# Preparing the first projection of a three-mixer block: modulation rows on the tensor engine, one rms pass, the low halves on VectorE

## The chip, the cores and the metric

The kernel runs on one core of one Trainium2 chip. The metric is the device time of one execution in microseconds; lower is better. Of three runs of the kernel before the median is 1512.63 us.

## The reference, cut to what matters

A block with attention is followed by two mixers (a gated convolution and an mLSTM). The change touches only the front end of the first block, where `x` is 512 x 1024 and `w_in` has 1024 rows:

```python
mod = c @ w_ada + b_ada                      # c: 1 x 1024, w_ada: 1024 x 3072
shift, scale, gate = split(mod, 3)
h = rms_norm(x, g_pre) * (1 + scale) + shift # per channel; rms per token
proj = h @ w_in
```

All is float32. A large product is made from three products of rounded halves: high x high, high x low, low x high. Every operand of such a product therefore has to be split into a high half (rounded by ScalarE) and a low half (value minus high half).

## The kernel before

`x` is held transposed: eight tiles of 128 channels by 512 tokens (`x1[:, k]`). For every tile `k` the kernel needs two columns of 128 numbers, `Gc[:, k]` = (1 + scale) * g_pre and `Sc[:, k]` = shift, and the inverse rms of each token, spread over all partitions (`rbc`, 128 x 512). From them comes the normalised tile `h`, split into `hh[:, k]` and `hl[:, k]` (in the trace `uh` and `ul`, whose memory they share).

*The modulation.* `ada_load(k)` fetches a 1 MB tile of `w_ada` (eight blocks of 128 x 256: 128 columns of scale beside 128 of shift) into one of three buffers `ada`. `ada_mac(k)` multiplies block `q` with the per-partition scalar `c` and adds up on VectorE: two TENSOR_SCALAR, six SCALAR_TENSOR_TENSOR and one TENSOR_TENSOR, all 128 x 256, into tiles `mac`. `modmm(k, m)` adds over partitions with two small matmuls against a column of ones, and two VectorE instructions make `Gc` and `Sc`.

*The rms.* `x` arrives in two halves of 256 tokens, four pieces each. For each half ScalarE squares eight tiles, VectorE adds them, `stat_cols` sums over partitions with matmuls, takes the root (ScalarE) and the reciprocal (VectorE), and `cols_bc` spreads the result by diagonal matrices and matmuls into `rbc`. Tiles 0 and 1 of `x` are multiplied by `rbc` on VectorE, tiles 2 to 7 on GpSimd.

*The tile.* `mkh(k)` runs ScalarE twice over the scaled tile (once rounding into `hh`, once exact into `t`), and VectorE subtracts to `hl`.

*The weights.* `Weights` streams units of the weights (here 128 x 768, 384 KB) into three buffers `wst`; `split_to` rounds a unit on ScalarE (`whi`) and subtracts for `wlo`, in this stage on GpSimd. For tile `k` the tensor engine then runs 18 matmuls: `hh` on `whi`, `hh` on `wlo`, `hl` on `whi`, six banks each, added up over the eight tiles.

*Warm-up.* Three calls of `warm` keep the tensor engine busy with products that nobody reads: 18 at the start, 14 and 6 around the rms.

*Order.* Nothing is issued as written. `Plan` collects every operation with its dependencies and costs and, when a phase ends, runs a simulation: each engine takes the ready operation that stands first in program order, and the instructions are issued in that order. The order on each engine is fixed from then on. The planner knows the ring of a tag (the next tile waits for the last one's users); it does not know of waits between pools.

*Pools.* Phases open pools over memory that earlier pools gave back: `sp2` follows `sp` and `cp`; `npool` and `sp3` follow `kvp` and `sp2`. By default an instruction that first writes into a new pool waits until the pools before it in that memory are done as a whole.

Of the kernel before, what the change touches and what calls it, by code (L numbers as in the profile page):

```python
# [31 lines left out]
V_C, V_GPRE, V_GPOST, V_NW0, V_NW1, V_FIN = 0, 8, 16, 24, 32, 40  # L32
# [398 lines left out]
def trunk(ctx, tc, a, out):  # L431
    nc = tc.nc
    plan = Plan(nc)
    V, A, G, PE, SP = plan.dve, plan.act, plan.pool, plan.pe, plan.sp

    def pool(stack, name, space=None):
        return Pool(stack.enter_context(tc.tile_pool(name=name, bufs=1, **({"space": space} if space else {}))))

    @contextmanager
    def phase():  # L440
# [37 lines left out]
    bank = Banks(pool(ctx, "psum", PSUM))  # L478
    W = Weights(plan, wpool, units, 3, 3)
# [14 lines left out]
    x1 = const.tile([128, KT, T], F32, name="x1")  # L494
    vec = const.tile([128, NV], F32, name="vec")
    SP.dma_start(vec, a["vec"])
    for h in range(0, S, 256):
        for k in range(0, KT, 2):
            SP.dma_start(x1[:, k:k + 2, META + h:META + h + 256], a["xT"][h // 256, :, k:k + 2])

    ident = const.tile([128, 128], F32, name="ident")
    plan.add("POOL", lambda: make_identity(nc, ident.real()), [], [ident], 0.6, 0.1)
    ones = const.tile([128, 128], F32, name="ones")
# [11 lines left out]
    def stat_cols(ss, n0, n, r, among=tuple(range(8)), early=False):  # L515


        nt = (n + 127) // 128
        full = n // 128
        sums = ss if isinstance(ss, list) else [ss]  # L520
        pcs = [bank((128, 8), among) for _ in range(nt if early else 1)]
        steps = [(t, e) for e in range(len(sums)) for t in range(nt)] if early else \
            [(t, e) for t in range(nt) for e in range(len(sums))]
        for t, e in steps:
            w = min(128, n - 128 * t)
            PE.matmul(pcs[t % len(pcs)][:w, t:t + 1], sums[e][:, n0 + t * 128:n0 + t * 128 + w], ones[:, 0:1],
                      start=(e == 0), stop=(e == len(sums) - 1))
        if early:
            parts = [(min(128, n - 128 * t), slice(t, t + 1)) for t in range(nt)]
        else:  # L530
            parts = [(128, slice(0, full))] if full else []
            if nt > full:
                V.memset(r[:, full:nt], 0.0)
                parts.append((n - 128 * full, slice(full, nt)))
        for w, c in parts:
            A.activation(r[:w, c], pcs[c.start % len(pcs)][:w, c], AF.Sqrt, bias=epsc[:w], scale=1.0 / D)
        for w, c in parts:
            V.reciprocal(r[:w, c], r[:w, c])

    def cols_bc(r, n, dg, outs, among=tuple(range(8))):  # L540

        pb = bank(among=among)
        for t in range(0, n, 128):
            w = min(128, n - t)
            V.tensor_scalar(dg[:w, t:t + w], ident[:w, :w], r[:w, t // 128:t // 128 + 1], 0.0, op0=OP.mult, op1=OP.add)
            PE.matmul(pb[:, t:t + w], ones[:w], dg[:w, t:t + w], start=True, stop=True)
        A.copy(outs[:, :n], pb[:, :n])
        return pb
# [85 lines left out]

    with phase() as sx:
        sp = pool(sx, "sp")
        acc = [bank(among=(i,)) for i in range(6)]
        ss = sp.tile([128, S], F32, name="ss")
        rbc = sp.tile([128, S], F32, name="rbc")
        adas = {}  # L640

# [3 lines left out]
        def ada_load(i, pieces=1):  # L645
            t = big(F32).rearrange("p (k c) -> p k c", k=KT)
            src = a["wada"][i].rearrange("p (k c) -> p k c", k=KT)
            n = KT // pieces
            for e in range(pieces):
                SP.dma_start(t[:, e * n:e * n + n], src[:, e * n:e * n + n])  # L650
            adas[i] = t

        def ada_mac(i):
            t = adas.pop(i)
            m = [sp.tile([128, 256], F32, name=f"mac{e}", tag=f"mac{e}", bufs=2) for e in range(2)]
            for e in range(2):
                V.tensor_scalar(m[e], t[:, e], vec[:, V_C + e:V_C + e + 1], 0.0, op0=OP.mult, op1=OP.add)
            for k in range(2, KT):
                V.scalar_tensor_tensor(m[k % 2], t[:, k], vec[:, V_C + k:V_C + k + 1], m[k % 2], op0=OP.mult, op1=OP.add)
            V.tensor_tensor(m[0], m[0], m[1], op=OP.add)  # L660
            return m[0]

        def modmm(k, m):
            pm = bank((128, 2), (6, 7))
            for j in range(2):
                PE.matmul(pm[:, j:j + 1], m[:, j * 128:j * 128 + 128], ones[:, 0:1], start=True, stop=True)
            V.tensor_scalar(Gc[:, k:k + 1], pm[:, 0:1], b1[:, k:k + 1], vec[:, V_GPRE + k:V_GPRE + k + 1],
                            op0=OP.add, op1=OP.mult)
            V.tensor_scalar(Sc[:, k:k + 1], pm[:, 1:2], vec[:, V_BADA + k:V_BADA + k + 1], 0.0,
                            op0=OP.add, op1=OP.add)  # L670

        def mkh(k):
            t = sp.tile([128, S], F32, name="ht", tag="ht", bufs=3)
            A.activation(hh[:, k], x1[:, k, META:], AF.Identity, bias=Sc[:, k:k + 1], scale=Gc[:, k:k + 1])
            A.activation(t, x1[:, k, META:], AF.Identity, bias=Sc[:, k:k + 1], scale=Gc[:, k:k + 1])
            V.tensor_tensor(hl[:, k], t, hh[:, k].bitcast(F32), op=OP.subtract)

        ada_load(0, 2)
        W.load_to(1)
        ada_load(1)  # L680
        W.load_to(2)
        ada_load(2)


        def warm(n, t):

            for _ in range(n):
                PE.matmul(acc[5][:, :128], ones, t, start=True, stop=True)

        warm(18, ones)  # L690
        W.split_to(1, G)
        prb = []
        for h in (slice(0, 256), slice(256, 512)):
            xh = slice(META + h.start, META + h.stop)
            for k in range(KT):
                sq = ss[:, h] if k == 0 else sp.tile([128, 256], F32, name="sq", tag=f"mac{k % 2}", bufs=2)
                A.activation(sq, x1[:, k, xh], AF.Square)
                if 0 < k < KT - 1:
                    V.tensor_tensor(ss[:, h], ss[:, h], sq, op=OP.add)
            rc0 = sp.tile([128, 2], F32, name="rc0", tag="rc0", bufs=2)  # L700
            stat_cols([ss[:, h], sq], 0, 256, rc0, (6, 7))
            if h.start:
                m = ada_mac(0)
            else:
                warm(14, rc0[:, 0:1].to_broadcast([128, 128]))
            prb = cols_bc(rc0, 256, sp.tile([128, S], F32, name="dg", tag="ht", bufs=3), rbc[:, h], (6, 7))
            for k in range(2):
                V.tensor_tensor(x1[:, k, xh], x1[:, k, xh], prb[:, :256] if h.start else rbc[:, h], op=OP.mult)
        modmm(0, m)
        warm(6, rbc[:, 256:384])  # L710
        mkh(0)
        modmm(1, ada_mac(1))
        mkh(1)
        for k in range(KT):
            if k + 3 < KT:
                ada_load(k + 3)
            W.load_to(k + 3)
            if k + 2 < KT:
                G.tensor_tensor(x1[:, k + 2, META:], x1[:, k + 2, META:], rbc, op=OP.mult)
                m = ada_mac(k + 2)  # L720
            W.split_to(k + 2, G if k + 1 < KT else None)
            wh, wl = W.parts.pop(k)
            W.used += 1
            for w, h in ((wh, hh), (wl, hh), (wh, hl)):
                for t in range(6):
                    PE.matmul(acc[t], w[:, t * 128:t * 128 + 128], h[:, k], start=(k == 0 and w is wh and h is hh),
                              stop=(k == KT - 1 and h is hl))
            if k + 2 < KT:
                modmm(k + 2, m)
                mkh(k + 2)  # L730
        W.split_to(W.used + 2)

        among = (2, 3, 4, 5, 0, 1)
# [6 lines left out]
        t = big(F32)  # L740
# [317 lines left out]
    with phase() as sx:  # L1058
# [44 lines left out]
            gate_mm(p, m)  # L1103
        for h in range(0, S, 256):
            for k in range(0, KT, 4):
                SP.dma_start(x1[:, k:k + 4, META + h:META + h + 256], a["xT"][h // 256, :, k:k + 4])
        SP.dma_start(x1[:, :, :META], a["metaT"].rearrange("(k p) t -> p k t", p=128))
        y = sp.tile([128, KT, S], F32, name="y")

# [568 lines left out]
def layout(inp):  # L1678
    g = {k: np.asarray(v) for k, v in inp.items()}
    f = np.float32  # L1680
    r = {}
    r["xT"] = np.ascontiguousarray(g["x"][0].reshape(2, 256, 8, 128).transpose(0, 3, 2, 1))
    r["metaT"] = np.ascontiguousarray(g["meta_tokens_2"].T)
    r["vec"] = np.ascontiguousarray(np.concatenate([
        _col(g["c"][0]), _col(g["g_pre"][0]), _col(g["g_post"][0]), _col(g["norm_w_2"][0]), _col(g["norm_w_2"][1]),
# [82 lines left out]
```

## Time and profile before

| | |
|---|---|
| median of three runs | 1512.63 us (1509.63 to 1514.08) |
| the profiled execution's own time | 1511.26 us |
| its span, first to last instruction | 1509.2 us |
| mean granted clock of the tensor engine | 0.983 |
| tensor engine (PE) busy | 1463.2 us, 97% |
| VectorE (DVE) busy | 880.3 us, 58% |
| ScalarE (ACT) busy | 606.4 us, 40% |
| GpSimd (POOL) busy | 248.2 us, 16% |

The profile is of one execution. Times in the trace run from the span's start. PEld is the weight load of the tensor engine, SP the engine that issues the DMAs. Busy time of VectorE and GpSimd includes time in which an instruction stands still on its way. The difference of 2.06 us between own time and span lies outside the instructions.

### The profile page before, as it was taken

To read this page: it belongs to the slowest core of one execution; us is meant where nothing else is said; L and a number is where in the kernel's file an instruction comes from. 1 tells how busy PE (TensorE), PEld (TensorE's weight loads), DVE (VectorE), ACT (ScalarE), POOL (GpSimd) and SP (SyncE) were. 2 spreads that over 40 slices of the span, in tenths; PEclk is the share of its full clock that TensorE was granted. 3 is DMA by queue.
4 is the path that set the end of the run, shared out by engine and by line. 5 is a ranking of instruction groups with operands and counts; after the bars stand their busy time and mean duration, and the time that the engine had idled before them with its cause. 6 is when DMAs were issued, how large, how long until landed. Compare 5 with 4: busy or idle time off the path is not lost.

```text
span 1509.2 us, 22556 instructions
## 1 busy us (share of the span) xinstructions
PE 1463.2 (97%) x8965; PEld 1300.1 (86%) x8965; DVE 880.3 (58%) x1710; ACT 606.4 (40%) x1103; POOL 248.2 (16%) x292
## 2 busy tenths in 40 slices
PE   5999999988999899999999999999999999999997
PEld 5787888856889899999999999988888888887886
DVE  7976758776558754454544545755534635453465
ACT  3475757772247422122212122554333333433333
POOL 3210323440002210011001001302002101100201
PEclk8999999989999999999999999999999999999998
DMA  6544121005445232222222222221222222222221
GB/s 232 181 130 149 58 83 43 15 1 183 154 137 171 71 98 85 98 85 98 85 89 94 91 93 79 97 84 55 89 81 84 70 98 71 70 98 83 72 70 56
DMA packets 44121, 142.60 MB, mean 94 GB/s; under 512 B 5745, under 2 KB 12145, under 8 KB 42609
## 3 DMA queue, kind: packets, MB, share of 16 engines
q1 hardware_dynamic: 44016, 141.17, 28.3%
q8 instruction: 70, 1.15, 0.3%
q14 instruction: 35, 0.28, 0.1%
HBM read 139.06 MB, written 2.10 MB: 94 GB/s over the span
## 4 chain that ended last, share of the span: by engine, by line
PE 74%; DVE 2%; DMA 0%; issue 0%; ACT 0%; DVEq 0%; ACTq 0%
PE bank L254 74%; DVE ul L254 0%; DVE y L254 0%; DVE wlo L254 0%; DMA ada<-in_wada 0%; DVE so L254 0%; DVE num L254 0%; DVE x L254 0%; DVE mg L254 0%; DVE ss L254 0%; DVE nss L254 0%; DVEq L1764 0%; ACT Dm L254 0%; DVE tb L254 0%; DVE rb L254 0%
## 5 line engine op out<-in xcount | busy, mean ns | idle before, releaser
L254 PE MATMUL bank<-ul,whi 128*128 128x264 f32 (+1 forms) x1784 | 570.8, 324 | 2.7 <-DVE ul L254 2.5
L254 PE MATMUL bank<-uh,whi 128*128 128x264 f32 (+1 forms) x1784 | 570.6, 325 | 2.2 <-ACT uh L254 2.2
L254 PE MATMUL bank<-uh,wlo 128*128 128x264 f32 (+1 forms) x1768 | 565.9, 324 | 0.0
L254 ACT CAST whi<-wst 128x1024 fp32r<-128x1024 f32 (+2 forms) x236 | 244.6, 1038 | 621.2 <-PE bank L254 452.1
L254 DVE TENSOR_TENSOR wlo<-wst,whi 128x1024 fp32r<-128x1024 f32 (+1 forms) x227 | 279.3, 1232 | 193.8 <-ACT whi L254 192.4
L254 PEld LDWEIGHTS bank<-ul,whi 128*128 128x128 f32 x1784 | 335.8, 188 | 28.9 <-DVE ul L254 4.0
L254 PEld LDWEIGHTS bank<-uh,whi 128*128 128x128 f32 x1784 | 335.4, 189 | 28.6 <-ACT uh L254 3.9
L254 PEld LDWEIGHTS bank<-uh,wlo 128*128 128x128 f32 x1768 | 333.4, 189 | 24.8 <-DVE wlo L254 0.4
L254 DVE TENSOR_TENSOR zr<-bank,rb 128x264 f32<-128x264 f32 (+1 forms) x64 | 35.8, 559 | 118.9 <-PE bank L254 118.9
L254 DVE TENSOR_TENSOR x<-x,bank 128x264 f32<-128x264 f32 (+2 forms) x102 | 49.9, 496 | 68.9 <-PE bank L254 67.4
L254 POOL TENSOR_TENSOR yv<-yv,rb 128x528 f32<-128x528 f32 x16 | 22.7, 1419 | 335.1 <-DVE yv L254 316.8
L254 PE MATMUL bank<-gh,wlo 128*128 128x264 f32 x256 | 72.5, 284 | 0.0
L254 PE MATMUL bank<-gl,whi 128*128 128x264 f32 x256 | 72.4, 283 | 0.0
L254 PE MATMUL bank<-gh,whi 128*128 128x264 f32 x256 | 72.3, 284 | 0.0
L254 POOL TENSOR_SCALAR P<-P,sm 128x256 f32<-128x256 f32 (+3 forms) x96 | 49.7, 536 | 84.4 <-DVE sm L254 38.2
L254 PE MATMUL bank<-whi,uh 128*128 128x512 f32 (+1 forms) x160 | 61.7, 386 | 0.3 <-DVE ak L254 0.3
L254 PE MATMUL bank<-wlo,uh 128*128 128x512 f32 (+1 forms) x160 | 61.7, 386 | 0.0
L254 PE MATMUL bank<-whi,ul 128*128 128x512 f32 (+1 forms) x160 | 61.6, 385 | 0.0
L254 ACT ACTIVATE P<-P,nm 128x256 f32<-128x256 f32 (+3 forms) x96 | 50.8, 530 | 7.4 <-DVE nm L254 6.1
L254 PE MATMUL bank<-Gh,whi 128*128 128x512 f32 (+1 forms) x144 | 53.5, 371 | 0.0
L254 PE MATMUL bank<-Gl,whi 128*128 128x512 f32 (+1 forms) x144 | 53.3, 370 | 0.0
L254 PE MATMUL bank<-Gh,wlo 128*128 128x512 f32 (+1 forms) x144 | 53.3, 370 | 0.0
(336 smaller groups left out, 2294.2 us busy)
## 6 DMA issues: line engine op xcount, KB each, us to landing
wst<-in_wci SPq DMA_DIRECT2D x64, 512.0 KB, 3.4
wst<-in_wqkv SPq DMA_DIRECT2D x32, 512.0 KB, 3.4
wst<-in_wzo SPq DMA_DIRECT2D x32, 512.0 KB, 3.4
wst<-in_wm SPq DMA_DIRECT2D x23, 512.0 KB, 3.4
ada<-in_wada SPq DMA_DIRECT2D x11, 1024.0 KB, 5.2
wst<-in_wout SPq DMA_DIRECT2D x16, 512.0 KB, 4.1
wst<-in_wco SPq DMA_DIRECT2D x16, 512.0 KB, 3.5
wst<-in_wmo SPq DMA_DIRECT2D x16, 512.0 KB, 3.4
```

The source lines that it names most:

```text
L254: call(*[v.real() if isinstance(v, View) else v for v in args], **{k: v.real() if isinstance(v, View) else v for k, v in kw.items()})
```

## The change

1. *Modulation.* For tiles 0, 1 and 4 `mod_pe` replaces `ada_mac` and `modmm`: eight float32 matmuls with one column of `c` as the stationary operand and a 128 x 256 block of `w_ada` moving, added up into one row of 256 in a bank of the pair (6, 7); ScalarE copies the row to SBUF; two matmuls turn it into columns; `mod_cols` is the same two VectorE instructions as before. Tiles 2, 3, 5, 6, 7 keep `ada_mac`.
2. *The rms.* One pass over 512 tokens; `x` arrives in four pieces of 512 KB; its layout in memory changes accordingly (also for the second load of `x` late in the block).
3. *The tile.* `x` is no longer scaled in place. `mkh` is now one VectorE instruction for `t = x * Gc * rbc`, one ScalarE instruction for `hh = t + Sc`, and one VectorE instruction for `hl = t + Sc - hh`.
4. *GpSimd.* It does nothing in this stage: the six multiplications by `rbc` go away, the low halves of the weights go to VectorE.
5. *Warm-up.* The first 18 products stay (on another bank), the 14 and the 6 are gone.
6. *Pools.* All pools are opened with `reuse_waits="tile"`: a first write waits for the users of the memory that its own tile covers, not for whole pools.

```diff
-        return Pool(stack.enter_context(tc.tile_pool(name=name, bufs=1, **({"space": space} if space else {}))))
+        return Pool(stack.enter_context(tc.tile_pool(name=name, bufs=1, reuse_waits="tile", **({"space": space} if space else {}))))
...
-    for h in range(0, S, 256):
-        for k in range(0, KT, 2):
-            SP.dma_start(x1[:, k:k + 2, META + h:META + h + 256], a["xT"][h // 256, :, k:k + 2])
+    for k in range(0, KT, 2):
+        SP.dma_start(x1[:, k:k + 2, META:], a["xT"][:, k:k + 2])
...
+        def mod_pe(k):
+            t = adas.pop(k)
+            pr = bank((1, 256), (6, 7))
+            for q in range(KT):
+                PE.matmul(pr, vec[:, V_C + q:V_C + q + 1], t[:, q], start=(q == 0), stop=(q == KT - 1))
+            row = sp.tile([1, 256], F32, name="row", tag="row", bufs=2)
+            A.copy(row, pr)
+            pm = bank((128, 2), (6, 7))
+            for j in range(2):
+                PE.matmul(pm[:, j:j + 1], row[:, j * 128:j * 128 + 128], ones[0:1, 0:1], start=True, stop=True)
+            mod_cols(k, pm)
...
         def mkh(k):
             t = sp.tile([128, S], F32, name="ht", tag="ht", bufs=3)
-            A.activation(hh[:, k], x1[:, k, META:], AF.Identity, bias=Sc[:, k:k + 1], scale=Gc[:, k:k + 1])
-            A.activation(t, x1[:, k, META:], AF.Identity, bias=Sc[:, k:k + 1], scale=Gc[:, k:k + 1])
-            V.tensor_tensor(hl[:, k], t, hh[:, k].bitcast(F32), op=OP.subtract)
+            V.scalar_tensor_tensor(t, x1[:, k, META:], Gc[:, k:k + 1], rbc, op0=OP.mult, op1=OP.mult)
+            A.activation(hh[:, k], t, AF.Identity, bias=Sc[:, k:k + 1])
+            V.scalar_tensor_tensor(hl[:, k], t, Sc[:, k:k + 1], hh[:, k].bitcast(F32), op0=OP.add, op1=OP.subtract)
...
+        ss = rbc
+        for k in range(KT):
+            sq = sp.tile([128, S], F32, name="sq", tag="ht", bufs=3) if k else ss
+            A.activation(sq, x1[:, k, META:], AF.Square)
+            if k:
+                V.tensor_tensor(ss, ss, sq, op=OP.add)
+        rc0 = sp.tile([128, 4], F32, name="rc0")
+        stat_cols(ss, 0, S, rc0, (6, 7))
+        cols_bc(rc0, S, sp.tile([128, S], F32, name="dg", tag="ht", bufs=3), rbc, (6, 7))
+        acc = [bank(among=(i,)) for i in range(6)]
+        ON_PE = (0, 1, 4)
...
+        mod(0)
+        W.split_to(1)
         mkh(0)
-        modmm(1, ada_mac(1))
+        mod(1)
         mkh(1)
         for k in range(KT):
             if k + 3 < KT:
                 ada_load(k + 3)
             W.load_to(k + 3)
+            W.split_to(k + 2)
             if k + 2 < KT:
-                G.tensor_tensor(x1[:, k + 2, META:], x1[:, k + 2, META:], rbc, op=OP.mult)
-                m = ada_mac(k + 2)
-            W.split_to(k + 2, G if k + 1 < KT else None)
+                mod(k + 2)
+                mkh(k + 2)
             ...
-            if k + 2 < KT:
-                modmm(k + 2, m)
-                mkh(k + 2)
```

## Rows read from the trace of the kernel before

**Rows 1.** The page's busy line for the whole span.

```profile
PE 1463.2 (97%) x8965; PEld 1300.1 (86%) x8965; DVE 880.3 (58%) x1710; ACT 606.4 (40%) x1103; POOL 248.2 (16%) x292
```

**Rows 2.** Windows, by stages: busy us of each engine, granted clock, DMA share, GB/s.

```profile
0.00:77.50 77.50, 59.21 (x277) 49.31 (x278) 61.67 (x130) 29.29 (x55) 24.94 (x20) 0.89 0.57 203
77.50:150.00 72.50, 70.80 (x363) 60.63 (x362) 52.50 (x83) 46.31 (x76) 8.40 (x10) 1.00 0.44 143
...
300.00:375.00 75.00, 64.63 (x281) 48.25 (x279) 53.37 (x175) 40.52 (x122) 21.43 (x47) 0.86 0.26 87
```

**Rows 3.** Timeline of the first stage: start, us, engine, instruction, [idle before, releaser].

```profile
23.21 0.37 ACT L254 COPY rbc<-bank 128x256 f32<-128x256 f32 x1 [3.32 <-PE bank L254]
...
24.72 0.81 ACT L254 ACTIVATE uh<-x,Sc,Gc 128x512 fp32r<-128x512 f32 x1 [0.40 <-DVE Sc L254]
25.00 9.64 DVE L254 SCALAR_TENSOR_TENSOR mac<-ada,vec,mac 128x256 f32<-128x256 f32 x6
...
36.79 0.99 PE L254 MATMUL bank<-ones,mac 128*128 128x1 f32 x4 [7.40 <-DVE mac L254]
...
66.81 2.45 DVE L254 SCALAR_TENSOR_TENSOR mac<-ada,vec,mac 128x256 f32<-128x256 f32 x6
...
71.47 0.81 ACT L254 ACTIVATE uh<-x,Sc,Gc 128x512 fp32r<-128x512 f32 x1 [2.26 <-DVE Sc L254]
...
76.11 1.52 PE L254 MATMUL bank<-ul,whi 128*128 128x512 f32 x6
```

**Rows 4.** Groups of instructions, 0 to 78 us: count, busy us, mean ns, idle before.

```profile
L254 DVE SCALAR_TENSOR_TENSOR mac<-ada,vec,mac 128x256 f32<-128x256 f32 x48 | 27.9, 638 | 0.0
L254 POOL TENSOR_TENSOR wlo<-wst,whi 128x768 fp32r<-128x768 f32 x8 | 16.1, 2016 | 38.7 <-ACT whi L254 38.7
...
L254 DVE TENSOR_SCALAR mac<-ada,vec 128x256 f32<-128x256 f32 x16 | 11.5, 749 | 0.0
...
L254 DVE TENSOR_TENSOR mac<-mac,mac 128x256 f32<-128x256 f32 x8 | 4.8, 603 | 0.1
...
L254 DVE TENSOR_SCALAR Gc<-bank,b,vec 128x1 f32<-128x1 f32 x8 | 2.2, 270 | 1.1 <-PE bank L254 1.1
...
L254 DVE TENSOR_TENSOR wlo<-wst,whi 128x816 fp32r<-128x816 f32 x2 | 2.0, 1003 | 0.8 <-ACT whi L254 0.8
```

**Rows 5.** Timeline of the start: the squares, the column sums, the diagonals' products.

```profile
10.02 0.42 ACT L254 ACTIVATE ss<-x 128x256 f32<-128x256 f32 x1 [1.97 <-DMA x<-in_xT]
...
12.34 0.71 ACT L254 ACTIVATE mac<-x 128x256 f32<-128x256 f32 x2
...
17.97 0.61 PE L254 MATMUL bank<-ht,ones 128*128 128x128 f32 x4
...
18.42 0.28 PE L254 MATMUL bank<-ones,ss 128*128 128x1 f32 x2
```

**Rows 6.** Group over the whole span that stands nearest to the new VectorE instructions.

```profile
L254 DVE SCALAR_TENSOR_TENSOR qs<-bank,r,qs 128x512 fp32r<-128x512 f32 x16 | 11.7, 751 | 5.5 <-ACT qs L254 5.0
```

**Rows 7.** Windows of two microseconds in the first stage, columns as in rows 2.

```profile
10.00:12.00 2.00, 0.00 (x0) 0.00 (x0) 0.85 (x2) 1.57 (x5) 0.00 (x0) 0.55 1.09 395
...
14.00:16.00 2.00, 2.00 (x11) 2.00 (x11) 2.00 (x8) 0.01 (x1) 0.00 (x0) 0.50 1.05 433
16.00:18.00 2.00, 2.00 (x16) 2.00 (x15) 1.34 (x4) 0.00 (x0) 0.00 (x0) 0.74 0.99 402
...
38.00:40.00 2.00, 2.00 (x6) 1.52 (x6) 1.97 (x7) 1.52 (x2) 0.00 (x0) 0.50 0.83 336
```

**Rows 8.** Timeline at the change of pools after the attention.

```profile
344.92 0.33 SPq L254 DMA_DIRECT2D ada<-in_wada  x1
344.96 0.06 DVE L254 MEMSET r<- 128x1 f32 x1 [2.44 <-POOL qs L254]
...
349.86 0.62 DVE L254 TENSOR_SCALAR mg<-ada,vec 128x256 f32<-128x256 f32 x2 [4.85 <-DMA ada<-in_wada]
...
353.25 0.50 PE L254 MATMUL bank<-qs,wlo 128*128 128x512 f32 x1 [1.73 <-DVE wlo L254]
```

More of the change, by code (lines that the diff above doesn't have):

```diff
@@ L636, in trunk @@
         sp = pool(sx, "sp")
-        acc = [bank(among=(i,)) for i in range(6)]
-        ss = sp.tile([128, S], F32, name="ss")
         rbc = sp.tile([128, S], F32, name="rbc")
@@ L661, in ada_mac, with mod_cols @@
             return m[0]
+        def mod_cols(k, pm):
+            V.tensor_scalar(Gc[:, k:k + 1], pm[:, 0:1], b1[:, k:k + 1], vec[:, V_GPRE + k:V_GPRE + k + 1],
+                            op0=OP.add, op1=OP.mult)
+            V.tensor_scalar(Sc[:, k:k + 1], pm[:, 1:2], vec[:, V_BADA + k:V_BADA + k + 1], 0.0,
+                            op0=OP.add, op1=OP.add)
         def modmm(k, m):
@@ L666, in modmm @@
                 PE.matmul(pm[:, j:j + 1], m[:, j * 128:j * 128 + 128], ones[:, 0:1], start=True, stop=True)
[L667 to L670, printed above, removed]
+            mod_cols(k, pm)
[9 more added lines that the diff above has]
+                PE.matmul(pm[:, j:j + 1], row[:, j * 128:j * 128 + 128], ones[0:1, 0:1], start=True, stop=True)
+            mod_cols(k, pm)
@@ L672, in mkh @@
         def mkh(k):
             t = sp.tile([128, S], F32, name="ht", tag="ht", bufs=3)
-            A.activation(hh[:, k], x1[:, k, META:], AF.Identity, bias=Sc[:, k:k + 1], scale=Gc[:, k:k + 1])
-            A.activation(t, x1[:, k, META:], AF.Identity, bias=Sc[:, k:k + 1], scale=Gc[:, k:k + 1])
-            V.tensor_tensor(hl[:, k], t, hh[:, k].bitcast(F32), op=OP.subtract)
[L678 to L703, printed above, removed]
-            else:
[L705 to L708, printed above, removed]
@@ L709, in trunk @@
-        modmm(0, m)
-        warm(6, rbc[:, 256:384])
+            V.scalar_tensor_tensor(t, x1[:, k, META:], Gc[:, k:k + 1], rbc, op0=OP.mult, op1=OP.mult)
+            A.activation(hh[:, k], t, AF.Identity, bias=Sc[:, k:k + 1])
+            V.scalar_tensor_tensor(hl[:, k], t, Sc[:, k:k + 1], hh[:, k].bitcast(F32), op0=OP.add, op1=OP.subtract)
+        for k in range(3):
+            ada_load(k)
+            W.load_to(k + 1)
+        wb = bank((128, 128), (6,))
+        for _ in range(18):
+            PE.matmul(wb, ones, ones, start=True, stop=True)
@@ L711, in trunk, with mod @@
+        def mod(k):
+            if k in ON_PE:
+                mod_pe(k)
+            else:
+                modmm(k, ada_mac(k))
+        mod(0)
+        W.split_to(1)
         mkh(0)
-        modmm(1, ada_mac(1))
+        mod(1)
         mkh(1)
@@ L1105, in trunk @@
             for k in range(0, KT, 4):
-                SP.dma_start(x1[:, k:k + 4, META + h:META + h + 256], a["xT"][h // 256, :, k:k + 4])
+                SP.dma_start(x1[:, k:k + 4, META + h:META + h + 256], a["xT"][:, k:k + 4, h:h + 256])
         SP.dma_start(x1[:, :, :META], a["metaT"].rearrange("(k p) t -> p k t", p=128))
@@ L1681, in layout @@
     r = {}
-    r["xT"] = np.ascontiguousarray(g["x"][0].reshape(2, 256, 8, 128).transpose(0, 3, 2, 1))
+    r["xT"] = np.ascontiguousarray(g["x"][0].reshape(512, 8, 128).transpose(2, 1, 0))
     r["metaT"] = np.ascontiguousarray(g["meta_tokens_2"].T)
```

## The prediction

> **What bounds the kernel now.** I read the page first. The tensor engine is busy for 97% of the span and no other engine for more than 58% [rows 1], so the kernel as a whole is bound by matmuls, and a change can win only where that engine stands idle or does work that nobody reads. The windows by stage show where this is: in the first 77.5 us it is busy for 59.2, and a part of that is warm-up; in the next 72.5 us for 70.8; later a hole of 10.4 us is left in the stretch from 300 to 375 [rows 2]. The change works on the first stage and, by its pools, on that hole.
>
> In the first stage the timeline is to be read for what the matmuls wait for. The inverse rms is written at 23.58, the first high half begins at 24.72, the last one at 71.47, and the last matmul ends at 77.63 [rows 3]. The 18 matmuls of a tile take some 4.2 us at full clock (six in 1.52 with the end of the last, so 1.4 from group to group), eight tiles 33.6. The stage is therefore 18 us longer than its products, counted from about 26 us on. Two things are to be seen. First, VectorE is busy without a pause: 61.7 us of 77.5 [rows 2], and its idle time lies in the prologue. Second, this busy time is inflated. Six SCALAR_TENSOR_TENSOR take 2.45 us at 66.81 and 9.64 us at 25.00, where GpSimd works beside them without a pause; the tensor engine then waits 7.40 us for the sum [rows 3]. At 0.41 us each, 48 of them would take 19.7 us; they took 27.9. The 16 TENSOR_SCALAR took 11.5; at 0.31 (two in 0.62, with GpSimd at rest [rows 8]) they would take 5.0. The eight sums took 4.8 for 3.3 [rows 4]. So 8.2 + 6.5 + 1.5 = 16.2 us of VectorE are standing beside GpSimd.
>
> **The change, part by part.** *VectorE's account.* Gone: the 16.2 us, since GpSimd rests; three `ada_mac` at 2 x 0.31 + 7 x 0.41 = 3.5, so 10.5; four scalings of half tiles, 1.7 at 0.42. Added: eight low halves of 128 x 768, at 1.0 for 816 columns [rows 4] 0.94 each, 7.5; eight `t` at 0.75, the row of a SCALAR_TENSOR_TENSOR of 128 x 512 with a pointer scalar [rows 6], 6.0; the form of `hl` costs some 0.06 more, 0.5. Seven additions of 512 take the place of twelve of 256, 4.8 for 5.1. Net 16.2 + 10.5 + 1.7 - 7.5 - 6.0 - 0.5 = 14.4 us less. With the idle time of before the stage would end at 77.6 - 14.4 = 63.2. That is a check; the path itself goes as follows.
>
> *Prologue.* The last pieces of `x` land between 10.0, where the second half's first square stops waiting, and 12.3, where the last squares no longer wait [rows 5]. Bytes and queue are the same in four pieces; I take 11.3. Two squares of 512 at 0.6 (two of 256 take 0.71 [rows 5]) and the last addition at 0.7 (0.75 with a pointer scalar [rows 6]) end at 13.2. From the column sums to `rbc` it took 5.2 us before (18.42 to 23.58 [rows 3, 5]), with VectorE held up; now there are four diagonals instead of two but nothing in the way. Bounds 3 and 5.2, taken 3.8: `rbc` at 17.0, 6.6 us earlier.
>
> *Row 0 on the tensor engine.* This is a new link in the chain. Its row needs a bank of the pair (6, 7), and the column sums hold it until the root has read them, about 14.8. Eight float32 matmuls are 16 instructions of 256 columns. No row has this shape. Nearest: four of 128 columns in 0.45 us at full clock (17.97 to 18.42 [rows 5]), 0.11 each, so 0.22 for 256 and 3.6 for a tile; at half clock 11 of 128 in 2 us [rows 7], 0.18, so 0.36 and 5.8 for a tile. Since the tensor engine will have been idle from 8 to 13, the clock starts low, as it did at 10 to 16 [rows 7], and rises under way: I take 4.7, and 1.0 for the diagonals' products between. The row is there at 20.5; copy 0.37 [rows 3], two matmuls of two instructions 0.5 [rows 5], `Gc` 0.27 [rows 4] and the handovers end at 22.0. So of the 6.6 us only some 2.5 reach the first tile. Row 1 stands behind row 0 in the queue and ahead of tile 0's products, which begin at 24.5.
>
> *From tile to tile.* VectorE then has, for a tile with `ada_mac`, 3.5 + 0.38 for the two columns (0.27 for the longer of them [rows 4], overlapping) + 0.94 + 1.5 = 6.3 us; for tiles 1 and 4 2.8. From 22.0: 1.5 for tile 0, 2.8, 6.3, 6.3, 2.8, 6.3, 6.3, and 5.6 to the last `t`: 37.9, less 1.5 us of tile 2's sum done while VectorE waits for row 0 (its 1 MB should have landed by then): so `t` of tile 7 ends at 58.4. From the start of its high half to the last matmul it takes what it took before, 6.16 (71.47 to 77.63 [rows 3]): 58.4 + 0.1 + 6.2 = 64.7. The tensor engine's own account gives nearly the same: 24.5 + 33.6 + five pairs of column sums at 0.5 + 4.1 for row 4 = 64.7. Both engines are then nearly full, so a little is lost between them: stage end 65.0, a gain of 12.6 us. ScalarE loses one pass of 0.8 per tile and gains three copies; it has 48 us idle in the stage [rows 2] and stays hidden.
>
> *Warm-up.* The 14 and 6 products filled waits; removing them frees nothing on the path. What they kept up is the clock (first rival).
>
> *Transfers.* All loads of the stage keep their order in SP's queue; `ada` tiles 0 and 1 now come free when the tensor engine has read them, others when VectorE has. At over 400 GB/s in the prologue [rows 7], 1.4 MB for a tile cost 3.5 us, below the 6.3. The second load of `x` is read in pieces of 256 numbers as it was already written; it lies under a full tensor engine. Both cost nothing.
>
> *Pools.* At 344.92 the load of a `w_ada` tile for the next phase starts only when GpSimd's last use of the old pool ends; VectorE, whose queue has that tile's products ahead of the next low half, waits 4.85 us, and the tensor engine then 1.73 for the low half [rows 8]. With waits by tile the load can start when the memory under it is free. If it starts 2 us earlier the 1.73 are gone; if it lies over the same late tile, nothing is. The rest of the 10.4 us hole is the end of the attention and its chain, which no pool makes wait. Taken 1.7, bounds 0 and 4.
>
> *After the stage.* Everything shifts as a block: the next stage is 98% full [rows 2]. The planner may order later queues differently since its simulated clocks differ; I set that to zero, 3 us either way, an estimate from the 1 to 2 us waits of the holes above.
>
> Sum against the profiled execution: 1511.26 - 12.6 - 1.7 = 1497.0 us, which is 15.6 below the median of the runs. About 0.3%, 4.5 us, is what this measurement can tell from no change.
>
> **Rivals.** *Half clock through the start.* The clock falls within the idle stretch at 10 to 12 and is at half until 16 to 18; at 38 to 40 whole products ran at half clock [rows 7]. If rows 0 and 1 run at half clock and tiles 0 and 1 as well, it costs 2 x 2.2 + 2 x 4.2 = 12.8, and the time is 1510, the same as before. Against it: tile 0 follows on two rows without a gap, and VectorE has room behind the early tiles. The Trainium skill speaks for it ("TensorE: Matmul & The Clock Gate", section "Why this matters for your kernels"): gaps between bursts of matmuls return the array to half its clock, so one should keep it busy, and this change takes warm-up out. By that rule the prologue's rows run slow; I have half of that in the sum. Chance 0.09.
>
> *GpSimd is not what stretches VectorE.* Then the five remaining sums keep 6 x 0.64 + 2 x 0.75 + 0.6 = 5.9 us each [rows 4], 2.4 more than 3.5, 12 us in all: 1509. Against it: the fast and the slow six at 66.81 and 25.00 [rows 3]. Chance 0.04.
>
> *Slower: a handshake in the queues.* `t` has moved to VectorE, so VectorE now needs `Gc`, and `Gc` needs two matmuls that stand in the tensor engine's fixed queue among 18 products. If the planner put them behind a tile's products, VectorE stands still up to 4.2 us for each of five tiles, with all that is queued behind: low halves and the next sum. 21 us give 1518. It turns the change into a loss above 2.9 us per tile. For it: the last high half waited 2.26 us for `Sc` before too [rows 3], though on an engine with time to spare. Against it: the queue is written from a simulation in which these matmuls stand first. Chance 0.07.
>
> *A larger gain.* `x` at 10.0, rows at full clock (1.1) and 4 us from the pools give 1497.0 - 1.3 - 1.1 - 2.3 = 1492; with later queues in its favour 1488. This is the low end; times below it have 0.1.
>
> **From cases to numbers.** The likeliest case, 1497 within its own bounds of 1490 to 1505, has 0.70; a larger gain 0.10; half clock 0.09; GpSimd innocent 0.04; handshake 0.07. The range for 8 in 10 runs from 1488, the low end, to 1507, where the cases near no change begin. Faster than 0.3% are the first two and a part of half clock: 0.84. The same: 0.09. Slower: 0.07.
>
> **What would show it.** `rbc` written near 17 and first `t` near 22; six SCALAR_TENSOR_TENSOR in 2.5 us everywhere in the stage; no wait of several microseconds before a column sum; the stage's last matmul at 62 to 68; the 1.73 us wait near 351 gone. The prediction is wrong if VectorE waits for the tensor engine between tiles, if the rows run at half clock and hold up tile 0 beyond 27, or if the holes after the attention grow.

## The result, and the profile after

The changed kernel takes 1497.2 us in the median of 4 runs (1496.9 to 1497.9), against 1513.4 for the kernel before in the 4 runs beside it. The ratio is 0.990, with a 95% interval of 0.9884 to 0.9917. The forecast was 1497.0. The profiled execution took 1497.03 us, 14.2 less than the profiled one of before; its span is 13.9 shorter, 1495.3 against 1509.2.

The page's busy line of the changed kernel, to be read beside [rows 1]:

```profile
PE 1463.4 (98%) x8965; PEld 1294.8 (87%) x8965; DVE 867.2 (58%) x1689; ACT 600.4 (40%) x1088; POOL 223.4 (15%) x278
```

Over the whole span hardly anything moved: VectorE has 13 us less, GpSimd 25 us less. Windows by stage, with the columns of [rows 2], show where it did. The first line is the first stage up to its last product, the second the next stage, the last the stretch of the first stage from its first product on:

```profile
0.00:65.65 65.65, 59.49 (x278) 43.98 (x279) 46.65 (x109) 23.09 (x40) 0.70 (x6) 0.97 0.67 242
65.65:138.00 72.35, 70.81 (x362) 60.53 (x362) 52.84 (x84) 46.21 (x76) 7.90 (x10) 1.00 0.43 142
...
24.28:65.65 41.37, 41.37 (x191) 31.81 (x191) 35.50 (x80) 12.04 (x17) 0.00 (x0) 1.00 0.54 187
```

The first stage ends at 65.65 instead of 77.63, 12.0 us earlier. VectorE is busy for 46.65 in it, not 61.67. The next stage is as full as before, so it shifts as a block. From its first product on the tensor engine has no idle time at all and full clock (41.37 of 41.37), and VectorE now has 5.9 us of rest: the two have changed places as the bound.

The timeline of the first stage answers to [rows 3, 5]:

```profile
9.39 1.15 ACT L254 ACTIVATE ht<-x 128x512 f32<-128x512 f32 x2 [0.25 <-DMA x<-in_xT]
...
12.13 1.02 PE L254 MATMUL bank<-ones,rbc 128*128 128x1 f32 x8 [4.24 <-DVE rbc L254]
13.20 0.26 ACT L254 ACTIVATE rc<-bank,epsc 128x4 f32<-128x4 f32 x1 [2.66 <-PE bank L254]
...
13.51 1.86 PE L254 MATMUL bank<-ada,vec 128*1 128x256 f32 x4 [0.35 <-ACT rc L254]
...
15.31 1.77 PE L254 MATMUL bank<-ht,ones 128*128 128x128 f32 x8
...
17.01 2.75 PE L254 MATMUL bank<-ada,vec 128*1 128x256 f32 x12
17.11 0.59 ACT L254 COPY rbc<-bank 128x512 f32<-128x512 f32 x1 [2.93 <-PE bank L254]
19.79 0.36 ACT L254 COPY row<-bank 1x256 f32<-1x256 f32 x1 [2.09 <-PE bank L254]
...
20.21 0.60 PE L254 MATMUL bank<-ones,row 1*128 1x1 f32 x4 [0.45 <-ACT row L254]
...
21.23 0.75 DVE L254 SCALAR_TENSOR_TENSOR ht<-x,Gc,rbc 128x512 f32<-128x512 f32 x1
...
24.28 1.66 PE L254 MATMUL bank<-uh,whi 128*128 128x512 f32 x6
...
64.13 1.52 PE L254 MATMUL bank<-ul,whi 128*128 128x512 f32 x6
```

To be seen: the last pieces of `x` land at 9.4, but the sums begin at 12.13, since the additions stand behind each other on VectorE. The root has read the bank at 13.46 and row 0 starts at once. Its first four instructions lie 0.43 us apart, the last twelve 0.22. The windows of two microseconds (columns of [rows 2]) say why, and show a second place far behind the stage:

```profile
10.00:12.00 2.00, 0.00 (x0) 0.00 (x0) 1.89 (x5) 0.54 (x2) 0.00 (x0) 1.00 0.96 390
12.00:14.00 2.00, 1.51 (x10) 1.16 (x11) 0.40 (x3) 0.80 (x2) 0.00 (x0) 0.80 1.06 437
14.00:16.00 2.00, 2.00 (x7) 0.84 (x6) 1.52 (x5) 0.18 (x1) 0.00 (x0) 0.50 1.03 416
16.00:18.00 2.00, 2.00 (x12) 1.30 (x12) 0.00 (x0) 0.59 (x1) 0.00 (x0) 0.85 0.99 413
...
252.00:254.00 2.00, 1.00 (x9) 0.81 (x7) 1.57 (x7) 2.00 (x5) 1.71 (x2) 1.00 0.00 0
254.00:256.00 2.00, 2.00 (x10) 1.75 (x11) 1.68 (x5) 1.79 (x5) 2.00 (x4) 0.89 0.00 0
256.00:258.00 2.00, 2.00 (x7) 1.51 (x7) 1.31 (x2) 0.36 (x1) 0.21 (x1) 0.50 0.00 0
```

After a rest of 4.24 us the granted clock falls between 12 and 14 (0.80) to its lower level, 0.50, and is back at full before 18 (0.85 from 16 on). The groups of the stage, to be read beside [rows 4]:

```profile
L254 DVE SCALAR_TENSOR_TENSOR mac<-ada,vec,mac 128x256 f32<-128x256 f32 x30 | 12.8, 478 | 0.0
...
L254 DVE TENSOR_TENSOR wlo<-wst,whi 128x768 fp32r<-128x768 f32 x8 | 7.6, 952 | 0.2 <-ACT whi L254 0.2
...
L254 DVE SCALAR_TENSOR_TENSOR ht<-x,Gc,rbc 128x512 f32<-128x512 f32 x8 | 6.0, 746 | 0.0
...
L254 DVE TENSOR_SCALAR mac<-ada,vec 128x256 f32<-128x256 f32 x10 | 3.1, 347 | 0.0
...
L254 DVE TENSOR_TENSOR mac<-mac,mac 128x256 f32<-128x256 f32 x5 | 2.1, 418 | 0.0
```

Without GpSimd beside them the three kinds of the sum take 478, 347 and 418 ns instead of 638, 749 and 603. At the change of pools (beside [rows 8]) the load is issued earlier, VectorE waits 2.77 us for it and not 4.85, and the tensor engine's product with the low half has no wait in front of it:

```profile
329.77 0.33 SPq L254 DMA_DIRECT2D ada<-in_wada  x1
...
334.60 0.62 DVE L254 TENSOR_SCALAR mg<-ada,vec 128x256 f32<-128x256 f32 x2 [2.77 <-DMA ada<-in_wada]
...
340.67 0.39 PE L254 MATMUL bank<-qs,wlo 128*128 128x512 f32 x1
```

Following the same matmul through both traces, the changed kernel is ahead by 12.0 us at the end of the stage, 12.25 near 134, 10.7 from 260 to 350, 12.8 behind the change of pools, and 12.9 from there to 1486. The last microsecond comes at the tail, where the clock was 0.60 and 0.50 before and is 0.94 now.

### The profile page after: what moved, and what is told of

Read it like the earlier page. It is cut to its first block, busy times and chain, and to the rows that moved or that the text cites. A ratio compares the mean times of both kernels' runs of the same rounds, so it can differ in the third digit from the quotient of the medians.

```text
span 1495.3 us, 22486 instructions
## 1 busy us (share of the span) xinstructions
PE 1463.4 (98%) x8965; PEld 1294.8 (87%) x8965; DVE 867.2 (58%) x1689; ACT 600.4 (40%) x1088; POOL 223.4 (15%) x278
## 3 DMA queue, kind: packets, MB, share of 16 engines
q8 instruction: 70, 1.15, 0.3%
## 4 chain that ended last, share of the span: by engine, by line
PE 93%; DVE 4%; ACT 1%; issue 1%; DMA 1%; POOL 0%; DVEq 0%; SPq 0%; ACTq 0%; POOLq 0%
PE bank L254 93%; DVE wlo L254 1%; DVE ul L254 0%; DVE y L254 0%; DVE P L254 0%; DMA x<-in_xT 0%; ACT whi L254 0%; DVE rbc L254 0%; POOL P L254 0%; DMA wst<-in_wm 0%; DVE zt L254 0%; DVE pl L254 0%; DVE ak L254 0%; DVE nm L254 0%; DVE so L254 0%
## 5 line engine op out<-in xcount | busy, mean ns | idle before, releaser
L254 DVE TENSOR_TENSOR wlo<-wst,whi 128x1024 fp32r<-128x1024 f32 (+2 forms) x235 | 286.9, 1222 | 196.3 <-ACT whi L254 194.6
```

Of the source, the lines that this page charges most:

```text
L254: call(*[v.real() if isinstance(v, View) else v for v in args], **{k: v.real() if isinstance(v, View) else v for k, v in kw.items()})
```

## The experiments

Eleven kernels were run. The products' columns are from the traces: start of the first product of the first stage, end of the last one, and the tensor engine's waits in between. Ratios are to the kernel before on the same chip.

| run | median us (range) | ratio, 95% interval | products from, to | waits |
|---|---|---|---|---|
| changed kernel | 1497.2 (1496.9-1497.9) | 0.990, 0.9884-0.9917 | 24.28, 65.65 | 0.0 |
| 1 pool waits of before | 1502.5 (1500.7-1504.1) | 0.994, 0.9916-0.9961 | 26.71, 68.08 | 0.0 |
| 2 low halves on GpSimd | 1502.2 (1500.0-1503.1) | 0.994, 0.9914-0.9956 | 25.63, 71.28 | 3.7 |
| 3 no rows on the tensor engine | 1499.2 (1498.1-1501.4) | 0.992, 0.9898-0.9941 | 21.59, 69.80 | 4.7 |
| 4 rows 0 and 1 only | 1498.3 (1496.8-1499.3) | 0.991, 0.9890-0.9938 | 25.89, 68.43 | 3.0 |
| 5 36 warm-up products | 1497.4 (1497.2-1497.6) | 0.991, 0.9888-0.9921 | 25.54, 66.90 | 0.0 |
| 6 rms in two halves | 1500.6 (1499.6-1501.1) | 0.993, 0.9911-0.9940 | 30.27, 71.49 | 0.0 |
| 7 before, pools by tile | 1509.0 (1506.8-1510.8) | 0.997, 0.9961-0.9983 | 26.84, 78.28 | 10.4 |
| 8 36 warm-up, own banks | 1495.8 (1492.5-1497.1) | 0.989, 0.9875-0.9908 | 21.82, 65.26 | 0.0 |
| 9 own banks | 1499.0 (1497.4-1500.3) | 0.992, 0.9907-0.9936 | 24.58, 68.01 | 0.0 |
| 10 first taps on ScalarE | 1494.8 (1494.2-1495.5) | 0.989, 0.9878-0.9911 | 21.78, 65.06 | 3.2 |
| 11 as 10, row 4 kept | 1494.7 (1493.2-1496.8) | 0.990, 0.9880-0.9909 | 22.31, 63.52 | 0.0 |

The start of the products moves by up to 2.4 us between executions of the same prologue (24.28 in the changed kernel, 26.71 in run 1), so lengths are compared beside ends. The clock goes with it: in run 1 it is at 0.50 from 12 to 20, and of the traces with this prologue the changed kernel's has the shortest such stretch. In runs 8 and 9 the planner put 12 products of the next stage in front of the last one, 2.3 us; their own length is 41.2. Of all intervals only that of run 7 lies clear of the changed kernel's, so what the other runs show is read from their traces. No run undoes the new form of `mkh` (part 3 of the change) by itself; its share isn't shown.

**Run 1: pool waits of before.**

```diff
-tc.tile_pool(name=name, bufs=1, reuse_waits="tile", ...)
+tc.tile_pool(name=name, bufs=1, ...)
```

> The changed kernel with pools opened as before, so that a first write waits for whole pools; nothing else is touched. Theory (pools by tile took away the wait for the low half after the attention): the load of the modulation tile starts again only when GpSimd's last product of the old pool ends, the wait of 1.7 us is back, and the kernel is slower by 1.7 to 2.4 us, all of it between the attention's end and the first products of the next phase; the first stage ends at the same 65.6 us. Rival (the place gained for another reason, such as another order of the queues): the time stays at 1497 within 0.5 us and no wait returns.

The stage keeps its length of 41.37. At the change of pools the waits are back, in the timeline:

```profile
339.93 0.62 DVE L254 TENSOR_SCALAR mg<-ada,vec 128x256 f32<-128x256 f32 x2 [5.15 <-DMA ada<-in_wada]
...
343.32 0.50 PE L254 MATMUL bank<-qs,wlo 128*128 128x512 f32 x1 [1.96 <-DVE wlo L254]
```

Same matmul against same matmul, it loses 2.4 us to the changed kernel there. The stage's end missed the expected 65.6, by the 2.4 us by which the products began later; 1.6 of them are made good near 257, where the changed kernel's clock fell and this one's did not. So ahead of the pools this execution is 0.4 behind, and at the tail, where its clock falls to 0.59 as it did before the change, it loses the rest of the 3.7 us between the spans. The medians are 5.3 apart, above the expected 2.4; what goes beyond the trace isn't explained.

**Run 2: low halves of the stage on GpSimd again.**

```diff
-        W.split_to(1)
+        W.split_to(1, G)
...
-            W.split_to(k + 2)
+            W.split_to(k + 2, G if k + 1 < KT else None)
```

> The changed kernel with the low halves of the first stage's weights on GpSimd again, as before. It takes eight instructions of 0.95 us off VectorE. Theory (GpSimd at work stretches VectorE's instructions beside it): eight instructions of about 2 us on GpSimd stretch VectorE by about two thirds of that, 10 us against the 7.6 saved; the 30 SCALAR_TENSOR_TENSOR of the modulation go from 478 ns to above 520 ns, and the stage ends 1 to 5 us later than 65.6, at 67 to 70. Rival (GpSimd is not what stretches VectorE): the instructions keep 478 ns, VectorE has 7.6 us less to do and the stage ends at 62 to 65.6, never later.

VectorE was relieved of eight instructions of 0.95 us and the products' stretch became 4.3 us longer (45.65 against 41.37). The group of the sums:

```profile
L254 DVE SCALAR_TENSOR_TENSOR mac<-ada,vec,mac 128x256 f32<-128x256 f32 x30 | 17.4, 633 | 0.0
```

Four rows of its timeline:

```profile
26.12 4.03 DVE L254 SCALAR_TENSOR_TENSOR mac<-ada,vec,mac 128x256 f32<-128x256 f32 x6
26.22 2.06 POOL L254 TENSOR_TENSOR wlo<-wst,whi 128x768 fp32r<-128x768 f32 x1 [2.10 <-ACT whi L254]
...
33.46 1.89 POOL L254 TENSOR_TENSOR wlo<-wst,whi 128x768 fp32r<-128x768 f32 x1 [5.18 <-ACT whi L254]
33.57 2.07 DVE L254 SCALAR_TENSOR_TENSOR mac<-ada,vec,mac 128x256 f32<-128x256 f32 x1
```

The last two are the cause itself. A VectorE instruction that takes 0.48 us alone starts 0.11 us behind one of GpSimd, takes 2.07 us, and ends 0.29 us after it. GpSimd's instruction holds one of VectorE's for its whole length. So it is with all eight in this trace: each holds one instruction of VectorE, which ends 0.08 to 0.55 us after it. Not only sums are held (the mean `t` goes from 746 to 1093 ns), and the products began 1.35 us later; the stage's end of 71.28 lies above the expected 70.

**Runs 3 and 4: fewer rows on the tensor engine.**

```diff
-        ON_PE = (0, 1, 4)
+        ON_PE = ()          # run 3
+        ON_PE = (0, 1)      # run 4
```

> The changed kernel with no modulation tile on the tensor engine: all eight are summed on VectorE as before the change, with GpSimd still at rest. Theory (both engines are nearly full, and the three rows relieve VectorE of 10.5 us while VectorE's wait of 5.3 us for row 0 goes away): the stage ends 2 to 6 us later than 65.6, at 68 to 72, with the tensor engine waiting between tiles. Rival A (the tensor engine alone is the bound, and the rows of 12 us in all are its burden): the stage ends earlier, at 58 to 64. Rival B (the rows are what the whole gain comes from): it ends at 75 or later.

> The changed kernel with tile 4 back on VectorE; tiles 0 and 1 stay as rows on the tensor engine. VectorE gets 3.5 us more, the tensor engine 3.6 less. Theory (both are nearly full from tile 2 on): the end moves by less than 2.5 us either way, 64 to 68, and some waits of the tensor engine for VectorE's sums appear. Rival (only VectorE is full): it ends 3.5 us later, at 69. Rival (only the tensor engine is full): 3.6 us earlier, at 62.

Without any row the first product starts 2.7 us earlier, at 21.59, since nothing stands between the diagonals and tile 0. But the products take 48.2 us, with waits of up to 2 us for the chain from a tile's sum over `Gc` and `t` to its high half, as here in run 3:

```profile
46.95 1.96 PE L254 MATMUL bank<-uh,whi 128*128 128x512 f32 x6 [1.96 <-ACT uh L254]
```

The stage ends 4.2 us later. The waits are 4.7 us; the granted clock is low as well, until 27 and again from 48 to 52 (0.53 and 0.62), and takes as much from the tensor engine as the waits, so the 4.2 aren't all the chain's. Row 4 alone is worth 1.2 (42.5 against 41.4); its end at 68.43 missed the expected 68, because the prologue was 1.6 later. None of the rivals holds. VectorE isn't full in either run (busy for 41.80 of 48.21 us in run 3 and 38.34 of 42.54 in run 4), and in run 4's longest wait, 1.59, a cast of weights stands ahead of the high half on ScalarE: `t` is ready at 40.19, the high half starts at 41.17.

**Runs 5, 8 and 9: warm-up and banks.** Run 8 is both edits, run 5 the first and run 9 the second alone.

```diff
-        for _ in range(18):
+        for _ in range(36):
             PE.matmul(wb, ones, ones, start=True, stop=True)
...
-            pr = bank((1, 256), (6, 7))
+            pr = bank((1, 256), (4,))   # row 0; pm in 5; row 1 in 2 and 3; acc taken after them
```

> The changed kernel with 36 instead of 18 warm-up products, so that the tensor engine is at work until about 11.9 us and not until 7.9. Theory: the half-clock stretch in the changed kernel's prologue (granted clock 0.80, 0.50 and 0.85 from 12 to 18 us) comes from its idle time of 4.2 us ahead of the column sums. With that filled the clock stays at full, eight column sums take 1.0, row 0 with the diagonals ends near 18, first t near 19.3, tile 0's products begin near 22.2 instead of 24.3; the products' length stays near 41.4, since the tensor engine sets it; stage end 63 to 64. Against the changed kernel 1.5 to 4 us less, 1493.5 to 1496. Rival (VectorE's account sets the stage, as the prediction's check by accounts has it): the start moves, the length grows by as much, the end stays at 65 to 66 and the time at 1497.

> The 36 warm-up products, and rows 0 and 1 get banks of their own (4, 5 and 2, 3) instead of the pair that holds the column sums. The prediction saw row 0 held up until the root has read that pair. Theory from the trace of the changed kernel: the tensor engine waited only 0.35 us for it, since w_ada's first tile lands at about the same time; so the stage ends within 0.6 us of the kernel with 36 warm-up products alone, and the time is within 1 us of it. Rival (the prediction's step): rows 0 and 1 start 1.5 to 2 us earlier and the stage ends that much earlier.

> The changed kernel with 18 warm-up products as it is, and banks of their own for rows 0 and 1. It tells which half of the run with 36 warm-up products and own banks brought tile 0 forward by 2.5 us. Theory: both are needed, since what costs is the half clock, and the clock falls when the tensor engine rests ahead of the column sums (4 us here) whatever the banks are; then a half-clock stretch stays between 12 and 20 us, row 0's matmuls run at 0.36 to 0.43 us a pair for a part of it, and tile 0's products begin between 23.5 and 25.5; time 1495.5 to 1498. Rival (the banks alone): with own banks the column sums and the rows follow without a rest, the clock is back at full by 14 us and tile 0 begins near 22; then the time is that of the run with both.

Windows of run 5, with the columns of [rows 2]:

```profile
14.00:16.00 2.00, 1.64 (x7) 0.50 (x6) 1.31 (x6) 1.00 (x2) 0.00 (x0) 0.68 0.98 403
16.00:18.00 2.00, 2.00 (x9) 1.70 (x8) 0.60 (x1) 0.00 (x0) 0.00 (x0) 0.50 1.04 434
```

The windows of run 8:

```profile
12.00:14.00 2.00, 1.93 (x13) 1.39 (x14) 0.46 (x3) 0.87 (x2) 0.00 (x0) 1.00 1.05 429
14.00:16.00 2.00, 2.00 (x14) 1.20 (x12) 1.46 (x5) 0.54 (x2) 0.00 (x0) 1.00 1.03 416
```

The windows of run 9:

```profile
12.00:14.00 2.00, 1.49 (x8) 1.52 (x8) 0.36 (x1) 0.00 (x0) 0.00 (x0) 0.50 1.05 431
14.00:16.00 2.00, 2.00 (x7) 0.78 (x8) 1.21 (x6) 0.98 (x2) 0.00 (x0) 0.50 1.02 415
```

Run 5 missed: the third piece of `x` landed at 9.26 in it, where the changed kernel's squares of that piece start at 8.00; the sums began at 13.22, a rest of 2.2 us was left ahead of them, and the clock fell between 14 and 16 (0.68). The rival's 1497 came out, but not its reason: the length stayed at 41.4. Run 9 has the half-clock stretch from 10 to 18 and starts its products at 24.58, as expected; its time of 1499.0 is 1 us above the expected range. Run 8 has full clock throughout the prologue, and its products start at 21.82, 2.5 us earlier than in the changed kernel. It was expected within 0.6 us of run 5's end and 1 us of its time; both are 1.6 us lower, since run 5 kept a half clock. The rival isn't tested by that, since of the 1.6 us by which row 0 starts earlier 1.15 are run 5's late `x`.

What the two edits are worth is seen from the first column sum to the first product, where the tensor engine issues the same 52 instructions in all these traces. Run 8 takes 9.75 us for them, without a wait. The changed kernel takes 12.15: 0.80 are waits for the pair of banks (0.35) and the copy of row 0 (0.45), the other 1.6 are the half clock. Run 9 takes 12.07 without a wait, so its banks do save the 0.8, and a longer half clock takes it back. Run 1, with the changed kernel's prologue, takes 14.41 with the same two waits. So the banks are worth 0.8 us there, and the half clock costs 1.6 to 3.9 by the execution.

Little of it reaches the end. In runs 8 and 9 the tensor engine waits 0.72 and 0.68 us right behind the stage for VectorE's copies of `ak`; same matmul against same matmul, of run 8's 2.5 us 0.9 are left near 80. Its trace is also its fastest run (1492.45, the others 1494.7 to 1497.1). Whether 36 products do without the banks when `x` is early isn't settled: run 5's trace fell on a late `x`, and its four runs agree within 0.4 us.

**Run 6: the rms in two halves.** The single pass is undone, with the eight loads of `x` and their layout.

```diff
-            A.activation(sq, x1[:, k, META:], AF.Square)
+    for h in (slice(0, 256), slice(256, 512)):  # loads, squares, sums, stat_cols, cols_bc
+            A.activation(sq, x1[:, k, META + h.start:META + h.stop], AF.Square)
```

> The changed kernel with the sum of squares in two halves of 256 tokens again (x loaded in eight pieces, two roots, two pairs of diagonals), all else as changed. Theory: the single pass contributes little, since the transfer of x and the additions behind it set the end of both forms; rbc 0 to 1.5 us later, stage end 65 to 68, time 1497 to 1499. Rival: the single pass is what brought the prologue forward; then rbc comes 4 to 6 us later, near 22, the stage ends at 70 or later and the time is above 1501.

Here my theory fell and the rival's place holds: `rbc` is written at 23.48, 5.8 us later, and the stage ends at 71.49. The timeline shows three reasons:

```profile
9.91 0.72 ACT L254 ACTIVATE ht<-x 128x256 f32<-128x256 f32 x2 [2.35 <-DMA x<-in_xT]
...
14.65 0.37 ACT L254 COPY rbc<-bank 128x256 f32<-128x256 f32 x1 [1.30 <-PE bank L254]
14.92 0.42 ACT L254 ACTIVATE ht<-x 128x256 f32<-128x256 f32 x1
...
17.83 1.02 PE L254 MATMUL bank<-ones,rbc 128*128 128x1 f32 x4 [3.21 <-DVE rbc L254]
...
19.20 2.72 PE L254 MATMUL bank<-ada,vec 128*1 128x256 f32 x6 [0.35 <-ACT rc L254]
```

Squares of the second half stand in ScalarE's queue behind the first half's copy, and the clock is at 0.50 from 12 to 22. The third isn't the edit's: the fourth of the eight pieces of `x` landed late, and the first half's sums begin at 11.46, where they began at 8.92 before the change, with the same eight pieces. So up to 2.4 of the 5.8 us can be this execution's. The time is 1500.6, just under the rival's 1501, as 1.6 us come back near 257 (last section).

**Run 7: the kernel before with pools by tile.**

```diff
-tc.tile_pool(name=name, bufs=1, ...)
+tc.tile_pool(name=name, bufs=1, reuse_waits="tile", ...)
```

> The kernel before with the pools' waits by tile alone. Theory: the pools' part is independent of the first stage and takes away the wait of 1.73 us for the low half near 351 and a little more: 1.7 to 2.4 us less than before. Rival: in the kernel before GpSimd's schedule holds the memory under the loaded tile anyway, so nothing changes there and the time is within 0.5 us of before; what the changed kernel gained there came from its shifted queues.

The wait of [rows 8] is gone. Same matmul against same matmul, it is 0.76 us behind right before the change of pools and 1.14 ahead after it: 1.9 us. (It was even near 200; a fall of the clock near 266 cost it 1.5, of which half had come back.) The timing says 2.6 to 5.9 (0.9961 to 0.9983 of 1513), above the expected 1.7 to 2.4. So the sign is shown twice and the size lies near 2 in the traces; what more the runs have isn't explained.

**Runs 10 and 11: a candidate.** ScalarE takes the first two products of each sum; 40 warm-up products and own banks; row 4 on VectorE (run 10) or on the tensor engine (run 11).

```diff
-                V.tensor_scalar(m[e], t[:, e], vec[:, V_C + e:V_C + e + 1], 0.0, ...)
+                A.activation(m[e], t[:, e], AF.Copy, scale=vec[:, V_C + e:V_C + e + 1])
```

> A candidate. From the runs so far: from tile 0 on the tensor engine is full in the changed kernel (144 products 34.3 us, row 4 3.6, sums and columns 3.1), and with row 4 back on VectorE it waits 3.0 us. Here rows 0 and 1 alone are on the tensor engine, and ScalarE (40 us idle in the stage) takes the first two products of each of the six sums, 0.62 us a tile from VectorE, 3.7 in all; with it 40 warm-up products and own banks for the rows. If both accounts are right, the stage's products take 37.5 to 39.5 us from a start near 22, the stage ends at 60 to 62 and the time is 1490 to 1494. If VectorE stays the limit (its waits hand back what it saves), the length is 41 or more and the time is that of the run with 36 warm-up products and own banks, 1495 to 1497.

> As the candidate, but with row 4 on the tensor engine as in the changed kernel. If the tensor engine is what sets the stage there, easing VectorE by another 3.1 us brings nothing against the run with 36 warm-up products and own banks: the products' length stays within 0.7 us of that run's and the time at 1494.5 to 1497. If VectorE's account sets it (the prediction's check by accounts), the stage is 2 to 3 us shorter and the time 1492 to 1494.

Run 11 tells most. VectorE's load in the products' stretch falls from 35.50 to 33.76 us, and the stretch stays at 41.21:

```profile
22.31:63.52 41.21, 41.21 (x190) 31.59 (x190) 33.76 (x73) 16.21 (x27) 0.00 (x0) 1.00 0.54 192
```

The tensor engine sets it, as expected of that case. Run 10 takes 3.6 us from the tensor engine, and waits of 3.2 come in their place, two of 1.59 for the high half:

```profile
31.66 0.83 ACT L254 CAST whi<-wst 128x768 fp32r<-128x768 f32 x1 [2.99 <-issue]
...
32.40 0.72 ACT L254 ACTIVATE uh<-ht,Sc 128x512 fp32r<-128x512 f32 x1
...
33.17 0.97 PE L254 MATMUL bank<-uh,whi 128*128 128x512 f32 x3 [1.59 <-ACT uh L254]
```

There a cast stands ahead of the high half in ScalarE's queue. Behind that wait the clock is low from 34 to 40 (0.70, 0.50, 0.95), which takes another 1.7 us. So the products take 43.3 us and not 37.5 to 39.5, and the expected 60 to 62 for the stage's end is missed (65.06). Every run of 10 and 11 is below every run of the changed kernel, by 2.5 us in the medians. But the kernel before was 2.4 us lower too beside them (1510.9, against 1513.4 beside the changed kernel), and the ratios agree within 0.001; so no gain over the changed kernel is shown.

## Why the prediction was right, step by step

- *VectorE's account.* Forecast 14.4 us less, measured 15.0 (61.67 to 46.65). The group means fell to those of GpSimd at rest, and run 2 brings one of them back (633 ns). The step is shown. What it did not say is the form: not a slower rate, but one instruction held for each of GpSimd's (run 2). The Trainium skill's page "SBUF — State Buffer", section "SBUF: two separate sides", has it: VectorE and GpSimd share a port pair as an exclusive lock, held for a whole instruction. The 2.07 us beside 1.89 agree.
- *Prologue.* `x` was taken at 11.3 and landed at 9.4; the last addition was taken at 13.2 and ended at 12.0. From the sums to `rbc` 3.8 was taken, with bounds 3 and 5.2; it took 5.6 (12.13 to 17.70), above the bound. The term was mis-sized by the half clock: in run 8 the same way takes 4.1 (12.07 to 16.19). "Nothing in the way" was wrong too: the diagonals are written by 14.66, and their products begin at 15.31, behind four slow instructions of row 0. That the two errors leave `rbc` at 17.7 for 17.0 is luck.
- *Row 0.* Right: 4.7 taken, 4.6 measured (1.86 and 2.75), partly at the lower clock, as assumed; the diagonals' products between took 1.7 for 1.0. First `t` at 21.23 for 22.0, tile 0 at 24.28 for 24.5. So near a hit belongs to this execution: runs 1 and 4, with the same prologue, begin tile 0 at 26.71 and 25.89. The bank was held until 13.46, not 14.8, and cost only 0.35.
- *From tile to tile.* The end of 65.0 came from two accounts of the same size. The tensor engine's was the one that counted: 41.4 us measured for 40.2, of which 34.3 are the 144 products at 0.238. VectorE's was not the limit: it rests for 5.9 us, and easing it (run 11) changes nothing. As soon as row 4 or all rows are taken away the tensor engine waits (runs 3 and 4), for a chain that runs through VectorE and ScalarE, with neither of them full.
- *Pools.* 1.7 taken; 2.1 in the changed kernel, 2.4 in run 1, 1.9 in run 7.
- *Later stages.* Zero taken, and the parts were not zero: 1.6 us lost near 257 and 1.0 won at the tail. 12.0 + 0.25 - 1.6 + 2.1 + 0.15 + 1.0 = 13.9, the difference of the spans. The mechanism and the size of the main term held; that the sum came within 0.2 us of the time is luck, since the stage gave 0.6 less than forecast and the pools 0.4 more, and the parts behind cancelled.
- *Rivals.* Half clock through the start is true for the prologue and false for the tiles: it ended before 18, ahead of tile 0. The rule of the Trainium skill's page "TensorE: Matmul & The Clock Gate", section "Why this matters for your kernels", that gaps between bursts put the array back to half its clock, agrees with the trace here: 0.50 behind the rest of 4.24 us. GpSimd innocent is refuted by run 2. The handshake didn't come: VectorE's longest wait for `Gc` behind the first is 0.68 us.

## What to carry to other kernels

Read an inflated group mean beside a second engine's timeline before moving work to that engine: here taking eight low halves back on VectorE shortened its own account. When two engines' accounts end at the same time, vary each alone; run 11, beside run 8, eases VectorE and leaves the stretch at 41.2, which says that the tensor engine counts. Work moved to the front of the tensor engine's queue also meets the clock that a rest left behind, so fill the rest: runs 8, 10 and 11, with rests of at most 0.5 us ahead of the sums, kept full clock through the prologue. Freeing the bank took away 0.8 us of waits, and a changed queue can give that back elsewhere: runs 8 and 9 did, behind the stage. Before a candidate is called faster, compare it with the kernel before as timed beside it.

## What was not expected of the hardware

The granted clock falls in some executions at two places far behind the change, and not in others of the same products: near 254 to 260 (the windows above) and near 496 to 516. The kernel before had such a rest too, at 264, without a fall; run 7, with the same products there, falls. First the kernel before, then the second window in run 7 and the one behind it:

```profile
264.00:266.00 2.00, 1.25 (x10) 1.04 (x8) 1.63 (x6) 1.98 (x5) 1.54 (x2) 1.00 0.00 0
266.00:268.00 2.00, 1.75 (x10) 1.57 (x11) 1.62 (x6) 2.00 (x5) 2.00 (x4) 1.00 0.00 0
```

```profile
266.00:268.00 2.00, 1.76 (x7) 1.48 (x8) 1.63 (x6) 2.00 (x5) 2.00 (x4) 0.68 0.00 0
268.00:270.00 2.00, 2.00 (x7) 1.69 (x6) 1.54 (x4) 0.02 (x1) 0.43 (x1) 0.50 0.01 4
```

Run 1 has 1.03 us of work in its window from 254 and keeps 1.00 behind it, and the changed kernel with 1.00 does not. A fall near 257 costs 1.6 us. In run 7 a longer fall near 510 takes back 1.4 us of what the pools gave in its trace. What decides isn't settled. Each such fall moves a span by about 1.5 us, so single traces of this kernel shouldn't be compared by spans that differ by less. A float32 matmul of one column of weights and 256 moving columns is two instructions of 0.22 us at full and 0.43 at half clock; 0.22 and 0.36 had been taken.
